# An encoder layer in three-pass fp32: output-projection digits and a merge on VectorE, weights of the down projection loaded straight into kept tiles, PSUM pools reordered

## The chip, the cores and the metric

One core of one Trainium2 chip. The metric is the device time of one execution in microseconds (us). TensorE multiplies, VectorE (DVE), ScalarE (ACT) and GpSimd (POOL) do the elementwise work, and SyncE (SP) issues most DMAs. Each engine takes its instructions strictly in its program's order; semaphores hold an instruction back until what it needs is there.

## What is computed

One layer (x is 1024 rows of 1024 channels, fp32):

```python
h = rmsnorm(x, g_mix)
z = h @ w_in                       # pooling channels | q | k | v
a = pool_mixer(z[pool]) @ w_branch_pool
b = diff_attention(q, k, v) @ w_branch_attn
gates = sigmoid(h @ w_gate + b_gate)
m = gates[pool] * a + gates[attention] * b
y = x + m @ w_out                  # output projection
f = rmsnorm(y, g_ffn)
out = y + relu(f @ w_up) ** 2 @ w_down     # up: 1024 -> 4096, down: 4096 -> 1024
```

## The kernel before

**Digits.** Every fp32 operand is split into two fp32r digits: ScalarE casts the high one (L135) and another engine subtracts it from the source for the low one (L136; VectorE unless the caller names GpSimd). A product is three matmuls in a row, high by high (L142), high by low (L143) and low by high (L144), in `mm3`.

**Seven products.** The large products use Strassen's scheme in Winograd's form: 2 x 2 blocks, seven products numbered "1" to "7", with sums of blocks (S, T, U) formed around them by `add` (L376) and `sub` (L379). Four stages matter here.

- Branch B (`b_product`, L1130 to L1142) makes the attention branch. Its results pass through `merge(d, th, k, eng)` (L1149 to L1153): the gates come in by DMA, ScalarE applies the sigmoid, VectorE multiplies (L1150), and `eng` adds the product to the half row in `mp` (the merged branches m, eight tiles). `merge(i, 1, U2[i], pool)`, four times, stands before the last product "4"; its rows read `mp<-mp,bU`.
- The output projection (`o_product`) multiplies the merged tiles, split into digits by `a_set` (L1158 high, L1159 low; rows `A<-mp`), by the weights. `w_set` loads a product's weights by two calls of `load_rows` (L175): 512 KB each into a raw tile `ro`, from a ring of two; each half is split into `wo`. A product has four such halves, so the seven products have 28 low digits `wo`. The results are in PSUM: oX (products 1, 6 and 3), oY (2 and 5) and oZ (7 and 4), four banks of each at a time. VectorE brings them out by `add` (`y<-oX`, `mp<-oX,xr` with the rows of x). Then come the norm of each row block (`nrs`, L232, L1294; L233 on GpSimd), the scaling `y` (L1299, L1301), the transposes `hb` by TensorE (L1310, eight to a row block, two PSUM banks hbN_0 and hbN_1) and ScalarE's copy out of PSUM (L1338), from which the digits of B11, B21 and the sums BT1 to BT4 are made.
- Up (`u_product`, PSUM tiles X, Y, Z, W) runs over pairs of column blocks of w_up (`wu`, 512 KB each, L1506). The sums `s` of weights (L376, L379) of the first pairs are made while the output projection still runs, and its first loads of `wu` are kept behind the loads of `ro` for products "7" and "4" by `issue_after`.
- Down (`d_product`, PSUM tiles Da and Db) takes quarter blocks: for each product and each q of 8 it loads `ur` (512 KB, L1682) and `wd` (512 KB, L1645), splits both (`u_0h`, `u_0l`, `w_0h`, `w_0l` and so on) and runs 24 matmuls of 128x512. Beside them two sums of weights are kept in SBUF: T1 = b12 - b11, made under product "1" and used in "5" and "6", and T2 = b22 - T1, made in "6" and used in "4". In `t1_made` a block `wdt` is loaded into the ring of raw weights and VectorE subtracts (L379, rows `T<-wdt,wd`), which frees both raw tiles. The raw tiles come from two rings, `prw0` with 2 and `prw1` with 4 tiles of 512 KB; `quarter` chooses between them.

**Order.** The code is traced in program order with priorities, and a list scheduler with a model of the engines writes each engine's final order; a changed engine or pool can therefore move neighbours. Tiles of a pool are reused in turn, and PSUM pools take the banks in the order in which they are opened. `pool_of(mlp_ps, ...)` opens up's PSUM pools after the output projection's banks have been given back.

Of the kernel before, what the change touches and what calls it, by code (L numbers as in the profile page):

```python
# [14 lines left out]
PSUM = bass.MemoryType.PSUM  # L15
# [52 lines left out]
def encoder_kernel(  # L68
# [21 lines left out]
    nc = tc.nc  # L90
# [36 lines left out]
    def raw(shape, name):  # L127
        return rpool.tile(shape, F32, tag="raw", name=name)

    def f(ap):  # L130
        return ap.bitcast(F32)

    def split(hi, lo, src, lo_eng=None):

        made = nc.scalar.copy(hi, src)  # L135
        (lo_eng or nc.vector).tensor_tensor(lo, src, f(hi), op=ALU.subtract)  # L136
        return made
# [34 lines left out]
    def load_rows(src, r0, c0, name, tile_fn):  # L172

        rw = raw([P, 2, 512], f"r{name}")
        loads[name[:2]] = nc.sync.dma_start(rw, src[r0 : r0 + 2 * P, c0 : c0 + 512].rearrange("(kk p) c -> p kk c", p=P))  # L175
        ws = []
        for j in range(2):
            w = tile_fn([P, 2, 512], f"w{name}_{j}")
            split(w[:, 0], w[:, 1], rw[:, j, :], nc.gpsimd)
            ws.append(w)  # L180
        return ws

# [11 lines left out]
    def gate(gts, c):  # L194
        for gt, c0, c1 in gts:
            nc.sync.dma_start(gt, g_dram[c * P : (c + 1) * P, c0:c1])
            nc.scalar.activation(gt, gt, AF.Sigmoid, bias=zero)
# [177 lines left out]
    def add(eng, out_, a, b):  # L375
        eng.tensor_tensor(out_, a, b, op=ALU.add)  # L376

    def sub(eng, out_, a, b):
        eng.tensor_tensor(out_, a, b, op=ALU.subtract)  # L379


    dve, pool = nc.vector, nc.gpsimd
# [38 lines left out]
    with ExitStack() as ph:  # L421
# [83 lines left out]
        act, dve, pol = nc.scalar, nc.vector, nc.gpsimd  # L505
# [487 lines left out]
        for g in range(-2, N + 10):  # L993
# [33 lines left out]
            for tok in ORDER:  # L1027
                if tok not in gens:
                    i = g - tok[1]
# [29 lines left out]
    def tmp(name):  # L1059
        nbank[1] += 1  # L1060
        return fr_tile([P, 512], name) if nbank[1] % 4 in (1, 2) else fo_tile(name)[:, 0:512]
# [24 lines left out]
    def half(d, th):  # L1086
        return mp[d][:, th * 512 : (th + 1) * 512]
# [46 lines left out]
    def b_product(ps, j, i):  # L1134
        c = slice(i * P, (i + 1) * P)
        for d in range(4):
            mm3(
                ps, wa[j][d][:, 0, c], wa[j][d][:, 1, c], *pair(by_[j][d]),
                j in "125" and d == 0, d == 3, j not in "125",
            )  # L1140

    def kept4(name):  # L1142
        ts = [hp0[0].tile([P, S], F32, tag="H", name=f"{name}{i}") for i in range(2)]
        return [ts[i // 2][:, i % 2 * 512 : (i % 2 + 1) * 512] for i in range(4)]

    def merge(d, th, k, eng):
        ga = tmp(f"ga{d}_{th}")
        gate([(ga, th * 512, (th + 1) * 512)], NK + d)
        out_ = ga if k.space == PSUM else k  # L1149
        nc.vector.tensor_tensor(out_, k, ga, op=ALU.mult)  # L1150
        add(eng, half(d, th), half(d, th), out_)
# [40 lines left out]
    U2 = kept4("bU2")  # L1192
# [18 lines left out]
    for i in range(4):  # L1211
        b_product(Z[i], "3", i)
        add(dve, U2[i], Z[i], U2[i])
        merge(i, 1, U2[i], pool)
    for i in range(4):
        b_product(X[i], "4", i)
        merge(i + 4, 0, X[i], dve)
# [8 lines left out]
    def pool_of(stack, name, bufs, space=None, side=None):  # L1226
        kw = {} if space is None else {"space": space}
        return stack.enter_context(
            tc.tile_pool(name=name, bufs=bufs, reuse_waits="tile", side=side, **kw)
        )  # L1230
# [23 lines left out]
    def w_set(j):  # L1254

        src, d0, dh = W_SRC[j]
        room = fw_tile if j in "67" else lambda shape, name: w_tile(shape, name, j not in "23")
        ws = []
        for d in (0, 2):
            ws += load_rows(src, (d0 + d) * P, dh * 512, f"o{j}_{d}", room)  # L1260
        return ws
# [126 lines left out]
    for step in O_TAIL.split():  # L1388
        t = int(step[1])
# [28 lines left out]
    es = pool_of(hs, "es", 2)  # L1418
    mlp_ps = ctx.enter_context(ExitStack())
    by = pool_of(mlp_ps, "by", 1, PSUM)  # L1420
    bm = pool_of(mlp_ps, "bm", 1, PSUM)
    bx = pool_of(mlp_ps, "bx", 1, PSUM)

    def ev(name, shape=(P, 512)):
        return e1.tile(list(shape), F32, tag="ev", name=name)
# [4 lines left out]
    T1s, T2_made = {}, {}  # L1430
# [196 lines left out]
    nraw = [0, 0]  # L1627
# [3 lines left out]
    wd = w_down.rearrange("(q i ab p) c -> ab p q i c", i=2, ab=2, p=P)  # L1631
    NQ = NP // 2
    T1s, T2s = {}, {}

    def kept(tag, q):
        return pd.tile([P, 2, 512], F32, tag=tag, name=f"{tag}_{q}", bufs=NQ)

    def keep(name):
        return pd.tile([P, 512], F32, tag="kp", name=name, bufs=12)

    def quarter(j, q, ab, dh):
        nraw[1] += j not in "1t"
        first = q % 4 < 2 if j == "1" else j != "t" and nraw[1] % 3 == 0
        r = prws[0 if first else 1].tile([P, 2, 512], F32, tag="rw", name=f"wd{j}_{q}_{ab}{dh}")
        nc.sync.dma_start(r, wd[ab, :, q, :, dh * 512 : (dh + 1) * 512])  # L1645
        return r

    def second(j, q):

        if j == "1":  # L1650
            b11[q] = quarter(j, q, 0, 0)
            return b11[q]
        if j == "5":
            return T1s[q]
        if j == "2":
            return quarter(j, q, 1, 0)
        if j == "3":
            return quarter(j, q, 1, 1)
        if j == "6":
            b22 = quarter(j, q, 1, 1)  # L1660
            T2s[q] = kept("T2", q)
            sub(dve, T2s[q], b22, T1s[q])
            return T2s[q]
        if j == "7":
            b22, b12 = quarter(j, q, 1, 1), quarter(j, q, 0, 1)
            sub(dve, b22, b22, b12)
            return b22
        b21 = quarter(j, q, 1, 0)
        sub(dve, b21, b21, T2s[q])
        return b21  # L1670

    b11 = {}

    def t1_made(q):
        b12 = quarter("t", q, 0, 1)
        T1s[q] = kept("T1", q)
        sub(dve, T1s[q], b12, b11.pop(q))

    def operands(j, q):
        nraw[0] += 1  # L1680
        ur = purs[nraw[0] > 2 and nraw[0] % 2].tile([P, 2, 512], F32, tag="ur", name=f"ur{j}_{q}")
        nc.sync.dma_start(ur, ud[SIDES[j][0], q])  # L1682
        out_ = []
        for n, src, pool_ in (("u", ur, puo), ("w", second(j, q), puo if (j, q) == ("1", 0) else pwo)):
            hi, lo = (pool_.tile([P, 2, 512], F32R, tag="op", name=f"{n}{j}_{q}{x}") for x in "hl")
            split(hi, lo, src, dve)
            out_ += [hi, lo]
        return out_
# [11 lines left out]
    def d_product(banks, j, last=False, early={}):  # L1700
        for q in range(NQ - 2 if last else NQ):
            d_step(banks, j, q, early.get(q) or operands(j, q), range(4))
            if j == "1" and q > 1:
                t1_made(q - 2)
        if j == "1":
            t1_made(NQ - 2)
            t1_made(NQ - 1)
        if last:
            ops = {q: operands(j, q) for q in (NQ - 2, NQ - 1)}
            for t in range(4):  # L1710
                for q in ops:
                    d_step(banks, j, q, ops[q], (t,))
# [6 lines left out]
    def with_residual(banks, name, th, dh):  # L1719

        got = []
        for t in range(4):
            k = keep(f"{name}{t}")
            add(dve, k, banks[t], residual(name, 4 * th + t, dh))
            got.append(k)
        return got
# [24 lines left out]
    U2 = with_residual(DX, "U2y", 0, 1)  # L1751
# [42 lines left out]
```

## Time and profile before

| | |
|---|---|
| median of 3 runs | 1525.06 us |
| lowest and highest | 1523.22, 1526.81 us |
| the profiled execution | 1526.86 us |
| its span in the trace | 1525.1 us |
| granted TensorE clock, mean | 0.999 |
| TensorE busy | 1510.0 us, 7590 matmuls and transposes |
| VectorE, ScalarE, GpSimd busy | 1063.1, 809.2, 405.9 us |
| DMA | 247.87 MB, mean 163 GB/s |

Busy times are shares of the span. TensorE's records are pipelined: a 128x512 matmul is listed with 0.39 us and follows the one before in 0.227. A bracket at a row's end gives the idle time of its engine ahead of it and what ended it. In the stage that the change begins with (about 795 to 875 us) the output projection runs, up starts at about 901, and down at about 1213. The last matmul ends at about 1521.

### The profile page before, as it was taken

The numbers are of one execution on the slowest core, as the hardware profiler recorded it, in microseconds if no ns is written. First come the engines' busy times: TensorE is split into PE (matmuls) and PEld (weight loads), VectorE is DVE, ScalarE is ACT, GpSimd is POOL, SyncE is SP. The second block draws the span as 40 slices with busy tenths as digits, with TensorE's granted clock in tenths as the row PEclk, the third lists the DMA queues.
The fourth block names the chain that finished last, engine by engine and source line by source line (L and its number), as shares of the span: only waits on it lengthen the run. The fifth ranks groups of instructions, "written<-read, shape, count | busy, mean of one in ns | idle before, by whom it ended". The sixth has DMA issues, their size and how long they took to land. (4 is left out here: it accounts for less than half of the span.)

```text
span 1525.1 us, 22082 instructions
## 1 busy us (share of the span) xinstructions
PE 1510.0 (99%) x7590; PEld 1308.3 (86%) x7590; DVE 1063.1 (70%) x2138; ACT 809.2 (53%) x1671; POOL 405.9 (27%) x489
## 2 busy tenths in 40 slices
PE   9999999999999999999999999999999999999999
PEld 8999998999999989888887778888888878888887
DVE  7777768887788777745469799667656668556572
ACT  7656565655555564554443477556555624333331
POOL 4545543454436343312447510000000000000000
PEclk9999999999999999999999999999999999999999
DMA  7224333422434244448855734454433899537650
GB/s 227 73 81 125 103 97 106 132 84 78 125 118 150 91 142 149 160 131 277 292 185 192 222 139 137 154 186 155 152 126 111 284 345 360 178 126 261 227 191 28
DMA packets 211211, 247.87 MB, mean 163 GB/s; under 512 B 12981, under 2 KB 146074, under 8 KB 211098
## 3 DMA queue, kind: packets, MB, share of 16 engines
q1 hardware_dynamic: 193530, 219.01, 43.7%
q10 hardware_dynamic: 17568, 27.44, 4.9%
q8 instruction: 60, 0.98, 0.3%
q14 instruction: 53, 0.43, 0.1%
HBM read 172.97 MB, written 73.43 MB: 162 GB/s over the span
## 5 line engine op out<-in xcount | busy, mean ns | idle before, releaser
L144 PE MATMUL z<-wqkv,hT 128*128 128x384 f32 x512 | 174.0, 340 | 0.1
L142 PE MATMUL z<-wqkv,hT 128*128 128x384 f32 x512 | 173.6, 340 | 0.1
L143 PE MATMUL z<-wqkv,hT 128*128 128x384 f32 x512 | 172.9, 338 | 0.0
L794 ACT ACTIVATE s<-s,nm 128x256 f32<-128x256 f32 (+7 forms) x128 | 99.4, 777 | 77.6 <-DVE nm L786 76.8
L716 POOL TENSOR_TENSOR ms<-ms,mhalf 128x4 f32<-128x4 f32 x64 | 71.0, 1110 | 164.7 <-DVE ms L715 160.6
L142 PE MATMUL g<-hT,fwgate 128*128 128x512 f32 x256 | 101.2, 395 | 0.6 <-ACT yps L340 0.4
L144 PE MATMUL g<-hT,fwgate 128*128 128x512 f32 x256 | 100.8, 394 | 0.0
L143 PE MATMUL g<-hT,fwgate 128*128 128x512 f32 x256 | 100.6, 393 | 0.0
L142 PEld LDWEIGHTS z<-wqkv,hT 128*128 128x128 f32 x512 | 96.3, 188 | 3.1 <-ACT hT L445 0.6
L143 PEld LDWEIGHTS z<-wqkv,hT 128*128 128x128 f32 x512 | 96.3, 188 | 2.5 <-DVE wqkv L445 0.3
L144 PEld LDWEIGHTS z<-wqkv,hT 128*128 128x128 f32 x512 | 96.2, 188 | 2.4 <-DVE hT L445 0.6
L786 DVE CUSTOM_DVE_ANT_0 s<-sc,dist 128x512 f32<-128x512 f32 (+3 forms) x128 | 71.8, 568 | 19.5 <-PE sc L784 13.9
L136 DVE TENSOR_TENSOR AS<-s,AS 128x512 fp32r<-128x512 f32 x64 | 43.5, 688 | 33.6 <-ACT AS L135 33.5
L783 PE MATMUL sc<-K,Q 128*128 128x512 f32 (+2 forms) x192 | 66.5, 351 | 0.2 <-DVE nm L786 0.2
L784 PE MATMUL sc<-K,Q 128*128 128x512 f32 (+2 forms) x192 | 65.0, 345 | 0.0
L136 POOL TENSOR_TENSOR wqkv<-rqkv,wqkv 128x384 fp32r<-128x384 f32 x56 | 58.7, 1067 | 23.5 <-ACT wqkv L135 23.2
L136 POOL TENSOR_TENSOR fwgate<-frgate,fwgate 128x512 fp32r<-128x512 f32 x32 | 43.7, 1367 | 58.6 <-ACT fwgate L135 58.5
L142 PEld LDWEIGHTS g<-hT,fwgate 128*128 128x128 f32 x256 | 48.1, 188 | 9.4 <-ACT yps L340 0.7
L144 PEld LDWEIGHTS g<-hT,fwgate 128*128 128x128 f32 x256 | 48.1, 188 | 9.2
L143 PEld LDWEIGHTS g<-hT,fwgate 128*128 128x128 f32 x256 | 48.1, 188 | 8.6
L136 DVE TENSOR_TENSOR AT_0l<-ta,AT_0h 128x512 fp32r<-128x512 f32 (+1 forms) x48 | 31.9, 666 | 30.1 <-ACT AT_0h L135 26.0
L379 POOL TENSOR_TENSOR wd<-wd 128x128 f32<-128x128 f32 (+1 forms) x64 | 50.3, 792 | 8.6 <-ACT wd L981 5.9
(513 smaller groups left out, 4670.6 us busy)
## 6 DMA issues: line engine op xcount, KB each, us to landing
wd<-in_w_down_dram SPq DMA_DIRECT2D x56, 512.0 KB, 5.2
wu<-in_w_up_dram SPq DMA_DIRECT2D x32, 512.0 KB, 4.3
udS<-us SPq DMA_DIRECT2D x64, 256.0 KB, 3.2
ur<-udS SPq DMA_DIRECT2D x32, 512.0 KB, 3.8
rqkv<-in_w_in_dram SPq DMA_DIRECT2D x64, 192.0 KB, 2.9
ur<-ud SPq DMA_DIRECT2D x24, 512.0 KB, 4.6
frgate<-in_w_gate_dram SPq DMA_DIRECT2D x32, 256.0 KB, 2.7
g_dram<-go ACTq DMA_DIRECT2D x32, 256.0 KB, 2.0
```

What stands on the lines that cost most here:

```text
L136: (lo_eng or nc.vector).tensor_tensor(lo, src, f(hi), op=ALU.subtract)
L142: nc.tensor.matmul(ps, lhs_hi, rhs_hi, start=first, stop=False, **kw)
L143: nc.tensor.matmul(ps, lhs_hi, rhs_lo, start=False, stop=False, **kw)
L144: return nc.tensor.matmul(ps, lhs_lo, rhs_hi, start=False, stop=last, **kw)
L379: eng.tensor_tensor(out_, a, b, op=ALU.subtract)
L716: powered[0] = nc.gpsimd.tensor_tensor(ms, ms, mhalf[:, 0:4], op=ALU.pow)
L783: nc.tensor.matmul(dst, Q[:, i, 0, :], rhs, start=True, stop=False)
L784: nc.tensor.matmul(dst, Q[:, i, 1, :], rhs, start=False, stop=True)
L786: nc.vector.tensor_tensor_reduce(out=s[i][:, c : c + w], in0=sc[:, 0:w], in1=dist[:, o0 + c : o0 + c + w], scale=2.0 ** -(h + 1), scalar=B ...
L794: exped[0] = nc.scalar.activation(s[i][:, 0:n], s[i][:, 0:n], AF.Exp, bias=last, scale=-1.0, accum_out=Z[:, i, t : t + 1])
```

## The change

Four edits:

1. `load_rows` names no engine for the low digits, so they go to VectorE.
2. `merge(i, 1, U2[i], ...)` adds on VectorE.
3. Up's PSUM pools are opened in the order by, bx, bm, where it was by, bm, bx.
4. In down, T1 and T2 are loaded straight into the kept tiles by a new helper `load_quarter`, and VectorE subtracts in place; the raw rings no longer hold a block for them, and `quarter` chooses its ring by another count.

```diff
@@ load_rows
-            split(w[:, 0], w[:, 1], rw[:, j, :], nc.gpsimd)
+            split(w[:, 0], w[:, 1], rw[:, j, :])
@@ branch B, product "3"
-        merge(i, 1, U2[i], pool)
+        merge(i, 1, U2[i], dve)
@@ PSUM pools of up
     by = pool_of(mlp_ps, "by", 1, PSUM)
+    bx = pool_of(mlp_ps, "bx", 1, PSUM)
     bm = pool_of(mlp_ps, "bm", 1, PSUM)
-    bx = pool_of(mlp_ps, "bx", 1, PSUM)
@@ down
+    def load_quarter(r, q, ab, dh):
+        nc.sync.dma_start(r, wd[ab, :, q, :, dh * 512 : (dh + 1) * 512])
+
     def quarter(j, q, ab, dh):
-        nraw[1] += j not in "1t"
-        first = q % 4 < 2 if j == "1" else j != "t" and nraw[1] % 3 == 0
+        nraw[1] += j != "1"
+        first = nraw[1] % 3 == 0 if j != "1" else q % 3 == 0
         r = prws[0 if first else 1].tile([P, 2, 512], F32, tag="rw", name=f"wd{j}_{q}_{ab}{dh}")
-        nc.sync.dma_start(r, wd[ab, :, q, :, dh * 512 : (dh + 1) * 512])
+        load_quarter(r, q, ab, dh)
         return r
@@ second, product "6"
-            b22 = quarter(j, q, 1, 1)
             T2s[q] = kept("T2", q)
-            sub(dve, T2s[q], b22, T1s[q])
+            load_quarter(T2s[q], q, 1, 1)
+            sub(dve, T2s[q], T2s[q], T1s[q])
@@ t1_made
-        b12 = quarter("t", q, 0, 1)
         T1s[q] = kept("T1", q)
-        sub(dve, T1s[q], b12, b11.pop(q))
+        load_quarter(T1s[q], q, 0, 1)
+        sub(dve, T1s[q], T1s[q], b11.pop(q))
```

In all 32 rows leave GpSimd's program and 32 join VectorE's; the other engines keep their number of rows. Up's banks are now X of the first product in bank 1, where it was bank 3; the transposes hb4 and hb5 use banks 0 to 3 in both.

On VectorE, in the middle of the output projection, the digits of product "5" and "3" (`wo5`, `wo3`) come between the digits of A for product "6" and the results of oY (the difference of the two orders):

```order
 L1159 TENSOR_TENSOR A6_2_9612<-mp2_8573,A6_2_9612 128x512
+L379 TENSOR_TENSOR mp7_8773<-mp7_8773,mp3_8605 128x512
+L136 TENSOR_TENSOR wo5_0_0_9688<-ro5_0_9686,wo5_0_0_9688 128x512
+L136 TENSOR_TENSOR wo5_0_1_9691<-ro5_0_9686,wo5_0_1_9691 128x512
 L1159 TENSOR_TENSOR A6_3_9615<-mp3_8605,A6_3_9615 128x512
+L136 TENSOR_TENSOR wo5_2_0_9696<-ro5_2_9694,wo5_2_0_9696 128x512
+L136 TENSOR_TENSOR wo5_2_1_9699<-ro5_2_9694,wo5_2_1_9699 128x512
 L376 TENSOR_TENSOR y0_9530<-oY0_9618,y0_9530 128x512
 L376 TENSOR_TENSOR y1_9545<-oY1_9635,y1_9545 128x512
 L376 TENSOR_TENSOR y2_9560<-oY2_9652,y2_9560 128x512
 L1159 TENSOR_TENSOR A5_0_9702<-mp0_8463,A5_0_9702 128x512
+L136 TENSOR_TENSOR wo3_0_0_9780<-ro3_0_9778,wo3_0_0_9780 128x512
```

Six rows (five new digits, and a sum that has moved down) now stand ahead of or between the additions `y<-oY` and the digits of A around them.

On TensorE, at the end of the output projection, the transposes of row block 4 (hb4) move behind the last product into oZ3:

```order
 L143 MATMUL oZ2_10084<-wo4_2_1_9907,A4_3_10007 128x512
 L144 MATMUL oZ2_10084<-wo4_2_1_9907,A4_3_10007 128x512
-L1310 MATMUL hb4_0_10216<-identf_95,y4_10135 128x128 x4
-L1310 MATMUL hb4_1_10217<-identf_95,y4_10135 128x128 x4
 L142 MATMUL oZ3_10162<-wo4_0_0_9896,A4_0_9998 128x512
 L143 MATMUL oZ3_10162<-wo4_0_0_9896,A4_0_9998 128x512
@@ -4517,4 +4515,6 @@
 L143 MATMUL oZ3_10162<-wo4_2_1_9907,A4_3_10007 128x512
 L144 MATMUL oZ3_10162<-wo4_2_1_9907,A4_3_10007 128x512
+L1310 MATMUL hb4_0_10216<-identf_95,y4_10135 128x128 x4
+L1310 MATMUL hb4_1_10217<-identf_95,y4_10135 128x128 x4
 L1310 MATMUL hb5_0_10256<-identf_95,y5_10194 128x128 x4
```

Now hb4 and hb5 stand together behind all of oZ's matmuls.

On SyncE, at the start of down, the queue before, behind the last `ur` of product "1":

```order
L1682 DMA ur1_7_13326<-ud11_7_10338 128x1024
L1716 DMA x1y00_13375<-yd_129 128x512
L1716 DMA x1y10_13379<-yd_129 128x512
L1716 DMA x1y20_13383<-yd_129 128x512
L1645 DMA wd1_4_00_13208<-in_w_down_dram 128x2x512
L1645 DMA wdt_2_01_13242<-in_w_down_dram 128x2x512
L1682 DMA ur2_0_13394<-ud12_0_10339 128x1024
L1645 DMA wd1_5_00_13248<-in_w_down_dram 128x2x512
L1645 DMA wdt_3_01_13282<-in_w_down_dram 128x2x512
L1682 DMA ur2_1_13430<-ud12_1_10340 128x1024
L1645 DMA wd1_6_00_13288<-in_w_down_dram 128x2x512
L1645 DMA wdt_4_01_13322<-in_w_down_dram 128x2x512
```

Each row `wdt` is a load for T1. The queue now, from the same row on:

```order
L1685 DMA ur1_7_13321<-ud11_7_10338 128x1024
L1642 DMA T1_0_13162<-in_w_down_dram 128x2x512
L1642 DMA T1_1_13201<-in_w_down_dram 128x2x512
L1642 DMA T1_2_13240<-in_w_down_dram 128x2x512
L1642 DMA T1_3_13279<-in_w_down_dram 128x2x512
L1642 DMA T1_4_13318<-in_w_down_dram 128x2x512
L1642 DMA T1_5_13357<-in_w_down_dram 128x2x512
L1642 DMA T1_6_13360<-in_w_down_dram 128x2x512
L1642 DMA T1_7_13363<-in_w_down_dram 128x2x512
L1719 DMA x1y00_13367<-yd_129 128x512
L1719 DMA x1y10_13371<-yd_129 128x512
L1642 DMA wd1_6_00_13284<-in_w_down_dram 128x2x512
```

The eight loads for T1 stand together, ahead of `wd1_6` (the seventh weight block of product "1"); `wd1_4` and `wd1_5` have moved ahead of this piece. Further down, the loads for T2 stand between those of product "2".

## The prediction

> **What bounds the kernel now.** The first part of the page comes first:
>
> ```profile
> PE 1510.0 (99%) x7590; PEld 1308.3 (86%) x7590; DVE 1063.1 (70%) x2138; ACT 809.2 (53%) x1671; POOL 405.9 (27%) x489
> ```
>
> TensorE is busy for all but 15 us of the span (1525.1 us), and the change leaves every matmul in the program. It can therefore win no more than the gaps between matmuls, and lose whatever new gap it makes. The list of TensorE's waits names the gaps (total us, times, longest):
>
> ```profile
> PE oX L142 <- DVE mp L376: 2.1, 2, 1.2
> PE Db L142 <- ACT w_0h L135: 1.9, 1, 1.9
> ...
> PE X L142 <- ACT y L1338: 1.0, 1, 1.0
> ...
> PE oY L142 <- ACT A L1158: 0.8, 1, 0.8
> PE oZ L142 <- DVE nrs L232: 0.6, 1, 0.6
> PE hb L1310 <- DVE y L1301: 0.5, 1, 0.5
> PE X L142 <- ACT U L1542: 0.5, 1, 0.5
> ...
> PE oY L144 <- DVE A L1159: 0.3, 1, 0.3
> ```
>
> Seven of these rows lie in 828 to 940 us, from the output projection (oX, oY, oZ) to the first products of up (X), and one is the first matmul of down's second product (Db). Only these are in the reach of the edits. The windows say what the other engines do there (columns: PE, PEld, DVE, ACT, POOL, clock, DMA share, GB/s):
>
> ```profile
> 800.00:900.00 100.00, 96.19 (x436) 77.76 (x435) 89.38 (x121) 46.60 (x95) 52.05 (x36) 1.00 0.59 195
> ...
> 1200.00:1300.00 100.00, 98.14 (x426) 80.74 (x426) 70.45 (x70) 42.35 (x49) 0.00 (x0) 0.98 0.93 337
> 1250.00:1260.00 10.00, 8.14 (x34) 6.30 (x33) 5.89 (x7) 3.86 (x4) 0.00 (x0) 0.93 1.00 353
> 1260.00:1270.00 10.00, 10.00 (x42) 8.19 (x40) 7.00 (x7) 4.03 (x5) 0.00 (x0) 0.90 1.03 384
> ```
>
> In the output projection VectorE is nearly full and GpSimd half busy; at the start of down the DMA engines are full (share 1.00) and every compute engine but TensorE has room. So the two halves of the change meet two different limits.
>
> A wait costs more than its row, because the first matmuls after it are slow to get going. TensorE's timeline around the first oX wait, and the start after the second:
>
> ```profile
> 849.65 0.39 PE L143 MATMUL oX<-wo,A 128*128 128x512 f32 x1
> ...
> 850.56 0.39 PE L144 MATMUL oX<-wo,A 128*128 128x512 f32 x1
> 851.82 0.47 PE L142 MATMUL oX<-wo,A 128*128 128x512 f32 x1 [0.88 <-DVE mp L376]
> 852.13 0.40 PE L143 MATMUL oX<-wo,A 128*128 128x512 f32 x1
> ...
> 864.16 0.47 PE L142 MATMUL oX<-wo,A 128*128 128x512 f32 x1 [1.21 <-DVE mp L376]
> ```
>
> Undisturbed, four spacings take 0.91 us, 0.227 each. From 850.56 to 852.13 two spacings take 1.57 instead of 0.45: 1.12 lost, 0.24 more than the 0.88 of the wait.
>
> **The digits and the merge (first two edits).** 28 low digits `wo` and 4 adds of the merge, 32 instructions of 128x512, go from GpSimd to VectorE. Their price is in the timelines of the two engines:
>
> ```profile
> 817.69 1.75 POOL L136 TENSOR_TENSOR wo<-ro,wo 128x512 fp32r<-128x512 f32 x1
> ```
>
> ```profile
> 818.21 1.78 DVE L1159 TENSOR_TENSOR A<-mp,A 128x512 fp32r<-128x512 f32 x1
> 819.91 0.68 DVE L1150 TENSOR_TENSOR ga<-bX,ga 128x512 f32<-128x512 f32 x1
> 820.51 0.68 DVE L379 TENSOR_TENSOR mp<-mp,mp 128x512 f32<-128x512 f32 x1
> ...
> 868.95 2.88 DVE L1159 TENSOR_TENSOR A<-mp,A 128x512 fp32r<-128x512 f32 x2
> ```
>
> With GpSimd idle such an instruction takes VectorE 0.60 us from start to start (819.91 to 820.51); beside a running `wo` of GpSimd it takes 1.70 (818.21 to 819.91) or 1.4 (the pair at 868.95). So VectorE gains 32 x 0.60 = 19.2 us of work, and each moved instruction takes away one of GpSimd's that could hold up VectorE by 0.8 to 1.1. GpSimd's 52 us in this window are some 30 instructions of 1.75; if two thirds of them meet a two-input operation of VectorE (my estimate), the hold-ups come to 16 to 22 us. VectorE's net load is then -3 to +3 us; I take 0. What does change is the order: a digit now is ready 0.60 us after ScalarE's high digit, not 1.75, and the two-slot ring of raw weights, which the low digit frees, turns faster. Three rows show that this ring paces the queue of SyncE, and through it VectorE and TensorE:
>
> ```profile
> SPq L175 <- POOL wo L136: 27.5, 10, 5.8
> ```
>
> ```profile
> 852.12 0.39 SPq L175 DMA_DIRECT2D ro<-o_sum  x1
> 852.56 0.46 SPq L1506 DMA_DIRECT2D wu<-in_w_up_dram  x1
> ...
> 853.78 0.51 SPq L1506 DMA_DIRECT2D wu<-in_w_up_dram  x1
> ```
>
> ```profile
> 851.00 0.68 DVE L376 TENSOR_TENSOR mp<-oX,xr 128x512 f32<-128x512 f32 x1
> ...
> 861.52 0.69 DVE L376 TENSOR_TENSOR s<-wu 128x512 f32<-128x512 f32 x1 [5.16 <-DMA wu<-in_w_up_dram]
> ```
>
> The load of `ro` at 852.12 stands ahead of up's first weights; the second `wu` leaves at 853.78, lands 7.7 us later, and VectorE stands 5.16 us before it with the eviction of oX in its queue behind it. That is the second oX wait. The first one is the eviction at 851.00, which stood behind digits of A that had been stretched. I followed the changed order row by row with 0.60 per instruction, the casts as before, and each DMA taking as long as before. VectorE then reaches the last digit of oY's first operand 2.3 us sooner than before, 1.2 ahead of its need; the eviction of oX that began at 851.00 begins at 845.1 where 848.8 is needed (850.79, when TensorE was through with what it had, less the 2 us won by then); `wu` leaves at 846 to 847 and lands by 855, so that the eviction behind it starts at 857.4 where 859.7 is needed (864.16 less the 1.37 lost there and the 3.1 won by then). Margins are 1 to 4 us. So oY's two waits, oX's two and oZ's go: 0.8 + 0.3 + 2.1 + 0.6 = 3.8, with 0.24 for each of six, 1.4: 5.2 us.
>
> **The PSUM order (third edit).** The transposes hb4 and hb5 keep PSUM banks 0 to 3, but X of up's first product leaves the bank that it shared with the last transposes (hb5_1, bank 3) for bank 1, that of hb4_1, which is given back sooner; the transposes hb4 and hb5 now stand behind all of oZ's matmuls. The waits of X on ACT y (1.0) and of hb on DVE y (0.5) should go with this and with the earlier y: 1.5 + 2 x 0.24 = 2.0. The wait of X on ACT U (0.5) has the same order as before and stays. By my replay the eviction of hb4_1 ends at 899 where X0 starts at 901.0, the thinnest place. Bounds: 0 if VectorE's chain of `y` is no earlier, 2.0 if it is. I take 1.5. Together with the digits: **6.7 us**, bounds 3 and 7.2.
>
> **Down (fourth edit).** No instruction goes or comes; the 8 + 8 loads of T1 and T2 no longer pass through the rings of raw weights, so they no longer wait for slots. The wait for them, before:
>
> ```profile
> 1226.06 8.21 DMA wd<-in_w_down_dram
> ...
> 1249.44 7.73 DMA wd<-in_w_down_dram
> ...
> 1258.29 1.89 PE Db L142 x4
> ```
>
> ```profile
> 1253.36 1.23 DVE L379 TENSOR_TENSOR T<-wdt,wd 128x1024 f32<-128x1024 f32 x1 [3.94 <-DMA wdt<-in_w_down_dram]
> ```
>
> ```profile
> 1256.05 0.39 PE L144 MATMUL Da<-w_7h,u_7l 128*128 128x512 f32 x1
> 1258.29 1.89 PE L142 MATMUL Db<-w_0h,u_0h 128*128 128x512 f32 x4 [1.86 <-ACT w_0h L135]
> ...
> 1262.74 0.39 PE L142 MATMUL Db<-w_0h,u_0h 128*128 128x512 f32 x1
> ```
>
> The chain runs load, digits, T, next load: the load of w_0 could leave only at 1249.44, as a T freed its slot. TensorE stops, and then runs slowly until 1262: from 1256.05 to 1262.74, 13 spacings take 6.69 where 13 x 0.227 = 2.95, so this place costs 3.74. Half of it is the clock, which the windows show granted at 0.93 and 0.90. [...]
>
> In the changed order SyncE issues all eight T1 loads in one row when the kept tiles come free (1223.4 in the time of before), ahead of the loads of w_6 and w_7 of the first product, and T2 loads stand between those of the second product. The engines carry 512 KB in 1.37 us at 384 GB/s, 1.49 at 353, 1.56 at 337 (rows above). A product's step of 24 matmuls takes 24 x 0.227 = 5.44, so the first product began 8 x 5.44 ahead of 1256.3, at 1212.8. Counting 512-KB units behind 1223.4, with some 2 us for the first to land: w_6 is the 11th, lands by 1241 and is needed with its digits by 1245.4; w_0 of the second product is the 17th or so, lands by 1250 and is needed at 1256.3; its w_1 is at 24.5 units, lands at 1258.9, 1261.8 or 1263.5 by the three rates, plus 1.05 for its cast, and is needed at 1261.7. So the wait of Db goes, and one at the next step takes its place: 0, 1.2 or 3.4 us. I take 1.2, of the middle rate, as both windows with full DMA engines bear it. Gain 3.74 - 1.2 = **2.5**, bounds 0 and 3.7.
>
> **Sum.** 6.7 + 2.5 = 9.2 us off the profiled execution's 1526.86, which is 1.8 above the median of the runs (1525.06) and within their spread; taken off the median: 1515.8. What moves less than 0.2% (3 us) a measurement of this kernel can hardly tell from no change.
>
> **Rivals.** (a) *The loads of T1 and T2 are in the way.* The DMA share of 1.00 speaks for it, and so does that 16 loads are pulled ahead of needed ones in one queue. [...] The count above has them in this order already, so it decides from 1.56 us a load: then w_1 costs 3.7 with its slow clock and down gains nothing: 1525.06 - 6.7 = 1518.4. Against it: 353 and 384 GB/s in the very place.
>
> (b) *The waits move on.* VectorE is at 89 of 100 us; if its net load is +3 and not 0, the margins of 1 to 2 us at oX and X0 are gone, two of the waits come back, and up's first steps wait for their digits instead: of the 6.7, 3 stay; with down's 2.5 minus up to 1: 1520.5. For it: the thin places. [...]
>
> (c) *The change does nothing that is seen:* the ring was not the pace, since `ro` lands late whoever frees it, and down's wait comes back one step on: within 3 us, 1524.
>
> (d) *Slower: VectorE takes over GpSimd's waits.* GpSimd stood idle ahead of its `wo` until ScalarE had a landed load to cast:
>
> ```profile
> 823.77 4.98 POOL L136 TENSOR_TENSOR wo<-ro,wo 128x512 fp32r<-128x512 f32 x3 [4.33 <-ACT wo L135]
> 832.82 6.41 POOL L136 TENSOR_TENSOR wo<-ro,wo 128x512 fp32r<-128x512 f32 x4 [4.07 <-ACT wo L135]
> ...
> 858.67 2.54 POOL L136 TENSOR_TENSOR wo<-ro,wo 128x512 fp32r<-128x512 f32 x2 [4.76 <-ACT wo L135]
> 864.86 6.42 POOL L136 TENSOR_TENSOR wo<-ro,wo 128x512 fp32r<-128x512 f32 x4 [3.64 <-ACT wo L135]
> ```
>
> Now the digit stands in VectorE's queue, and behind it the evictions that free oX and oY for TensorE. If the four waits of 16.8 us in all come over, and each has 2 us of margin, 8.8 us of gaps appear and the 6.7 don't go: 1525.06 + 8.8 - 2.5 = 1531.4. It decides where a `ro` lands more than 11 us after its issue, not 7.7 as the `wu` beside it did, or where the order has a digit ahead of an eviction that is due before it. Against it: in the replay ScalarE's cast comes before VectorE reaches the digit in all places but those with margin.
>
> **How the numbers follow.** Forecast 0.50, (a) 0.13, (b) 0.17, (c) 0.10, (d) 0.10. Faster by over 0.2% is the forecast with (a) and (b), 0.80; the same is (c), 0.10; slower is (d), 0.10. The range leaves out (c) and (d): its low end has all bounds at their best (7.2 + 3.7, and 1 us of run to run, 1513.2), its high end is (b) with down's gain gone, 1522.
>
> **What would show it.** Right: in the profile after, the list of TensorE's waits has lost oX <- mp, oY, oZ, hb and X <- y; GpSimd has no row between 800 and 870 but the nrs; VectorE's L1159 rows are 0.68 throughout; the `s<-wu` of 861.52 has no wait over 2 us; Db <- w_0h is gone and a shorter Db <- w_1h stands there. Wrong: VectorE waiting on ACT wo or on DMA ro with oX <- mp behind it (d); a wait of Da or Db for w_6h or w_1h of over 3 us (a); new waits for digits of up between 900 and 950 (b). A time over 1522 would mean that one of these took a size that no row here gives.

## The result and the profile after

The changed kernel takes 1515.70 us (median of 6 runs, 1514.81 to 1516.14), the kernel before 1524.16 us (6 runs, 1522.84 to 1526.81). The ratio is 0.9943, with a 95% interval of 0.9930 to 0.9955: 8.5 us faster. The forecast was 1515.8 us. The span of the profiled execution fell from 1525.1 to 1514.1 us, by 11.0, more than the times did; why, the last experiment shows: the profile before was of an execution with larger waits than most.

The list of TensorE's waits in the changed kernel, its first three rows (total us, times, longest):

```profile
PE warm L445 <- POOL inv L215: 1.1, 1, 1.1
PE ta L839 <- DVE AT L136: 0.8, 1, 0.8
PE X L142 <- ACT U L1542: 0.4, 1, 0.4
```

The first two lie before 560 us and stood in the kernel before too, among the rows of its list that were left out. Of the eight rows that the prediction lists from the output projection, up and down, one is left, X <- ACT U, the one whose order the change did not touch. The windows (PE, PEld, DVE, ACT, POOL, clock, DMA share, GB/s):

```profile
800.00:900.00 100.00, 100.00 (x466) 83.25 (x465) 93.40 (x165) 51.61 (x113) 4.68 (x8) 1.00 0.61 208
...
1200.00:1300.00 100.00, 100.00 (x442) 82.79 (x442) 76.36 (x73) 42.96 (x46) 0.00 (x0) 1.00 0.93 351
1220.00:1230.00 10.00, 10.00 (x46) 8.28 (x45) 8.61 (x8) 2.11 (x2) 0.00 (x0) 1.00 1.04 404
1250.00:1260.00 10.00, 10.00 (x46) 8.28 (x45) 10.00 (x10) 5.13 (x5) 0.00 (x0) 1.00 1.04 413
```

From 800 to 900 VectorE now executes 165 instructions, 44 more, in 4 us more of busy time (93.40 for 89.38). At the start of down the DMA engines move 404 to 413 GB/s. VectorE's timeline in the output projection:

```profile
820.17 0.69 DVE L1159 TENSOR_TENSOR A<-mp,A 128x512 fp32r<-128x512 f32 x1
...
828.59 1.89 DVE L1159 TENSOR_TENSOR A<-mp,A 128x512 fp32r<-128x512 f32 x3
...
843.83 0.68 DVE L376 TENSOR_TENSOR mp<-oX,xr 128x512 f32<-128x512 f32 x1
...
854.24 0.69 DVE L376 TENSOR_TENSOR s<-wu 128x512 f32<-128x512 f32 x1 [1.72 <-DMA wu<-in_w_up_dram]
```

The digits of A (L1159) follow each other in 0.60 us, three take 1.89, and from 818 us on none takes 1.78 any more. The first copy `mp<-oX,xr` starts 7.2 us sooner than before, `s<-wu` 7.3 us sooner, with a wait of 1.72 in place of 5.16. At the start of down:

```profile
1216.57 4.57 SPq L1642 DMA_DIRECT2D T<-in_w_down_dram  x8
```

```profile
1251.27 1.06 ACT L135 CAST w_1h<-wd 128x1024 fp32r<-128x1024 f32 x1 [5.92 <-DMA wd<-in_w_down_dram]
```

```profile
1253.51 1.22 DVE L136 TENSOR_TENSOR w_1l<-wd,w_1h 128x1024 fp32r<-128x1024 f32 x1
```

```profile
1254.45 1.07 PE L142 MATMUL Db<-w_1h,u_1h 128*128 128x512 f32 x4
1255.36 0.39 PE L143 MATMUL Db<-w_1l,u_1h 128*128 128x512 f32 x1
```

The eight loads of T1 leave in one row. The block w_1 of the second product, at which a new wait was forecast, is cast over at 1252.3; its first matmul runs at 1254.5, without a wait. Its low digit is over at 1254.7 and is needed at 1255.4, because four matmuls with the high digit come first. So w_1 is in time by 0.6 us only.

### The profile page after: what moved, and what is told of

Same layout as the page of the kernel before. It is cut to its first block, busy times and chain, and to the rows that moved or that the text cites. A ratio compares the mean times of both kernels' runs of the same rounds, so it can differ in the third digit from the quotient of the medians.

```text
span 1514.1 us, 22055 instructions
## 1 busy us (share of the span) xinstructions
PE 1506.0 (99%) x7590; PEld 1308.1 (86%) x7590; DVE 1062.3 (70%) x2170; ACT 809.3 (53%) x1671; POOL 352.5 (23%) x457
## 4 chain that ended last, share of the span: by engine, by line
PE 96%; DMA 1%; ACT 1%; DVE 1%; issue 1%; SPq 0%; POOL 0%; DVEq 0%; ACTq 0%; POOLq 0%
PE z L144 5%; PE z L142 5%; PE z L143 5%; PE Da L143 4%; PE Da L142 4%; PE Da L144 4%; PE g L142 4%; PE g L144 4%; PE g L143 4%; PE X L142 3%; PE X L144 3%; PE Db L143 3%; PE Db L142 3%; PE X L143 3%; PE Db L144 3%; PE sc L783 2%
```

## The experiments

Two lengths of the trace tell where a kernel gains or loses: from the first matmul of oX to the first of X on B11 (output projection to up), and from the first of Da to the first of Db on w_1 (down's first product and one step of the second). Neither depends on when the stage began. What a kernel loses in a stage is its length less that of the changed kernel (84.5 and 49.0 us). The times come from four sets of runs, in which the kernel before had medians of 1524.16, 1524.30, 1523.75 and 1523.40 us; between rows of different sets, less than 1 us says nothing. Each ratio below is to the kernel before in the same set.

| kernel | time, us | oX to X, us | Da to Db's w_1, us |
|---|---|---|---|
| before, first profile | 1524.16 | 92.0 | 52.7 |
| before, second profile | 1524.24 (one run) | 90.6 | 51.4 |
| changed | 1515.70 | 84.5 | 49.0 |
| digits alone | 1517.93 | 85.3 | 49.6 |
| merge alone | 1523.29 | 90.6 | 50.3 |
| PSUM order alone | 1523.30 | 90.1 | 50.8 |
| down alone | 1522.63 | 90.7 | 49.0 |
| changed, GpSimd busy | 1531.78 | 100.1 | 49.0 |
| changed, two more loads | 1521.02 | 84.5 | 54.4 |
| changed, T1 straight only | 1515.41 | 84.5 | 49.0 |
| changed, T2 straight only | 1529.88 | 84.5 | 62.5 |
| before, wu earlier | 1521.25 | 88.5 | 53.5 |
| changed, PSUM order of before | 1516.66 | 85.3 | 49.0 |

### The edits one by one

Each of four kernels has one edit of the diff and nothing else.

> The first edit alone: the 28 low digits wo on VectorE, all else as before. My theory: GpSimd's reads no longer hold up VectorE's two-input operations, so the waits of oY, oX and oZ go, some 5.2 us of gaps in TensorE's timeline, and with the earlier y the wait of hb too (0.7); X <- ACT y (1.0 us and its 0.24) and Db <- w_0h (3.7 with the slow clock) stay. Time 5 to 6 us under the kernel before. Rival, the digits in VectorE's own queue do the harm that the other edits hide: under 3 us gained. Rival, the four adds of the merge matter too: one of the two oY waits stays, 4 us gained.

Measured: 1517.93 us, ratio 0.9957 (0.9942 to 0.9972), 6.4 us under the 1524.30 that the kernel before took beside it. All waits of oY, oX, oZ and hb are gone. What is left in the list:

```profile
PE X L142 <- ACT y L1338: 0.7, 1, 0.7
...
PE Db L143 <- DVE w_0l L136: 0.3, 1, 0.3
```

The wait of X stays, shorter. The wait of Db did not stay at 1.9 as expected: here it is 0.3 for the low digit, though SyncE's order of down is that of the kernel before. So the first edit alone is worth most of the whole.

> The second edit alone: four adds of the merge on VectorE. My theory: they lie at 803 to 818 us, where TensorE did not wait, and GpSimd goes on with the digits; VectorE gets 2.4 us more work and about as much less hold-up, the waits of oY and oX stay within 0.5 us of what they were: no change, within 1 us. Rival, the adds ran on the path to the first digits of oY's operand: the oY waits go, 2 us gained.

Measured: 1523.29 us, ratio 0.9997 (0.9988 to 1.0006). No change, as expected; the waits of oY (0.8) and oX (1.4) are there.

> The third edit alone: only the PSUM banks of up's tiles change, every engine's order is that of before. My theory: the wait of X on ACT y (1.0 us, 1.26 with its restart) goes, as X no longer stands behind the last copy out of hb5_1; nothing else changes: 1 to 1.3 us gained in the trace, which the times can hardly show. Rival, the copies out of hb and VectorE's y are late by themselves: the wait comes back in the next product of up, nothing gained.

Measured: 1523.30 us, ratio 0.9991 (0.9982 to 1.0001). X <- ACT y is gone from the list, and nothing came in its place; from oX to X it takes 0.6 us less than the kernel with the merge alone, and 0.5 less than the second profile of the kernel before. The times can't tell it from no change.

> The fourth edit alone: T1 and T2 loaded straight into the kept tiles. My theory: the wait of Db for w_0h and the slow clock behind it go, 3.7 us, and no other wait comes in its place as the loads now run at over 400 GB/s; the seven waits of the output projection stay. Time 3.7 us under the kernel before. Rival, the gain in the kernel with all edits came through down's earlier start: a wait of Db stays here, under 2 us gained.

Measured: 1522.63 us, ratio 0.9989 (0.9980 to 0.9999): 1.7 us, half of what was expected. In the trace no wait of Da or Db is left, and the length is 49.0 us: nine steps of 5.44, all that can be had. The kernels without this edit show 49.6 to 53.5 there, in most of them less than in the first profile (52.7).

### Are VectorE's hold-ups the cause, or the ring of raw weights?

The digits' move does two things: GpSimd hardly works beside VectorE any more (busy 52.05 us of 100 before, 4.68 after, from 800 to 900), and the ring is freed sooner. This kernel leaves the low digits on VectorE, as the changed kernel does, and brings GpSimd's work back. It has all edits, and additions on GpSimd whose results nobody reads.

```diff
+    spare = pr1.tile([P, 2, 512], F32, tag="rw", name="spare")
+    nc.gpsimd.memset(spare[:, 0], 0.0)
...
             ws += load_rows(src, (d0 + d) * P, dh * 512, f"o{j}_{d}", room)
+            for _ in range(2):
+                add(pool, spare[:, 1], spare[:, 0], spare[:, 0])
```

> The changed kernel with 28 additions of 128x512 on GpSimd, from about 800 us on, that nobody waits for (they read and write a spare raw tile of up). Hold-ups theory (GpSimd's reads of SBUF hold up VectorE's instructions with two inputs in SBUF): with the digits now on VectorE too, each addition of 1.3 to 1.75 us costs VectorE 0.8 to 1.1, 22 to 30 us in all between 800 and 850; VectorE was 93% full there, so oY and oX wait for it again, at least the 5 us of the kernel before are lost: 1521 us or more. Rival, what counted was only that the ring of raw weights is given back sooner: the time stays within 1 us of the changed kernel's 1515.7.

Measured: 1531.78 us, ratio 1.0053 (1.0038 to 1.0068), 16 us over the changed kernel. TensorE's list, and the two engines' timelines:

```profile
PE oX L142 <- DVE mp L376: 4.0, 1, 4.0
PE oY L144 <- DVE A L1159: 3.8, 1, 3.8
PE oY L142 <- ACT A L1158: 2.7, 1, 2.7
```

```profile
816.21 39.42 POOL L376 TENSOR_TENSOR spare<-spare 128x512 f32<-128x512 f32 x28
```

```profile
819.48 1.52 DVE L376 TENSOR_TENSOR mp<-mp,ga 128x512 f32<-128x512 f32 x1
820.92 1.53 DVE L136 TENSOR_TENSOR wo<-ro,wo 128x512 fp32r<-128x512 f32 x1
822.37 1.52 DVE L1159 TENSOR_TENSOR A<-mp,A 128x512 fp32r<-128x512 f32 x1
823.82 1.52 DVE L379 TENSOR_TENSOR mp<-mp 128x512 f32<-128x512 f32 x1
825.27 0.68 DVE L1150 TENSOR_TENSOR ga<-bX,ga 128x512 f32<-128x512 f32 x1
825.87 0.92 DVE L136 TENSOR_TENSOR wo<-ro,wo 128x512 fp32r<-128x512 f32 x1
```

While GpSimd adds, VectorE's instructions with two inputs in SBUF start 1.45 us apart, not 0.60; the one with an input in PSUM (825.27) keeps its 0.60, and the one right behind it (825.87) takes 0.84. The waits of oY and oX come back, larger than in the kernel before. VectorE now has the digits as well, and GpSimd adds without a pause; which of the two makes them larger was not tested. Beside such a stream the digits on VectorE do not pay.

The experiment does not hold the ring fixed: as VectorE makes the digits later, two loads of `ro` that leave at 833.5 and 835.3 in the changed kernel leave at 848.2 and 852.5 here. But the trace keeps the two apart. VectorE has no idle time over 0.06 us from 795.4 to 854.3, past both waits of oY, so it waited for no load; and the waits end with digits of A and a copy out of oX, not with a `wo`. The same holds in the kernel before: from 812.2 to 841.5 VectorE stands still only once, for 0.14 us, and oY's waits (829.4 and 830.7) lie in that time. So the rival that only the ring counted does not hold for oY's waits.

That the ring and SyncE's queue count too, the next kernel shows. It is the kernel before, with up's first loads released by the first load for product 7:

```diff
+            loads.setdefault(f"first{j}", loads[f"o{j}"])
...
-                    later.enter_context(tc.issue_after(loads["o4" if p else "o7"].ins))
+                    later.enter_context(tc.issue_after(loads["o4" if p else "first7"].ins))
```

> The kernel before, with up's first two loads kept behind the first load of ro for product 7 and no longer behind the second: they leave some 7 us sooner, as in the changed kernel, while the digits stay on GpSimd. Theory: the second wait of oX (0.5 to 1.2 us) came from VectorE standing before wu with the copy out of oX behind it, so it goes or falls under 0.3; the first wait of oX and those of oY come from held-up digits and stay: 0.7 to 1.5 us less of gaps in the trace, within the spread of the times. Rival, both oX waits come from held-up digits alone: both stay.

Measured: 1521.25 us, ratio 0.9984 (0.9975 to 0.9994). Its list:

```profile
PE Db L142 <- ACT w_0h L135: 2.6, 1, 2.6
...
PE oX L142 <- DVE mp L376: 0.9, 1, 0.9
...
PE oY L142 <- ACT A L1158: 0.8, 1, 0.8
```

```profile
852.90 0.92 DVE L376 TENSOR_TENSOR s<-wu 128x512 f32<-128x512 f32 x1 [0.19 <-DMA wu<-in_w_up_dram]
```

One wait of oX is left of two. VectorE's `s<-wu` waits 0.19 us here, 5.16 before; the scheduler also put that instruction five places sooner, which the experiment could not keep apart from the load. The first wait of oX and oY's stay, with GpSimd's digits. The waits of oZ (0.6) and hb (0.5) are not in this list either, and X <- ACT y is 0.7 and not 1.0. So the earlier load, with the place of `s<-wu`, takes the second oX wait and the later waits of oZ and hb away, though GpSimd still makes the digits: 2.1 of the 5.2 us that the digits' move gives between oX and X (88.5 and 85.3, against 90.6 in the second profile of the kernel before). The waits that stay, oY's and the first of oX, are left to the hold-ups; no kernel here takes away the hold-ups alone.

### Which loads matter in down

> The changed kernel with T1 loaded straight, T2's block loaded through the ring of raw weights as before. Theory: only T1's loads held the ring where TensorE waited (Db <- w_0h), so the time is that of the changed kernel within 1 us and no wait of Db or Da is listed. Rival, T2's loads matter: a wait of 0.5 us or more comes in the second product or in the sixth.

The edit against the changed kernel:

```diff
+            b22 = quarter(j, q, 1, 1)
             T2s[q] = kept("T2", q)
-            load_quarter(T2s[q], q, 1, 1)
-            sub(dve, T2s[q], T2s[q], T1s[q])
+            sub(dve, T2s[q], b22, T1s[q])
```

Measured: 1515.41 us (1515.27 to 1515.68), no wait of Da or Db. T1 alone does it, and no kernel of these is faster than the changed one by more than the times can tell. With T2 back in the ring, w_1 is cast over 8.9 us before its first matmul; in the changed kernel it was 2.1. So T2's straight loads gain nothing here and take up the margin at w_1.

> The changed kernel with T2 loaded straight, T1's block through the ring with the ring's choice as before. Theory: Db waits for w_0h or w_0l as in the kernels without the fourth edit, 0.3 to 1.9 us, and the time is 0.5 to 2.5 us over the changed kernel's. Rival: the ring's pressure comes from T2's loads; no wait, same time as the changed kernel.

The edit against the changed kernel (and the rule of `quarter` as before):

```diff
+        b12 = quarter("t", q, 0, 1)
         T1s[q] = kept("T1", q)
-        load_quarter(T1s[q], q, 0, 1)
-        sub(dve, T1s[q], T1s[q], b11.pop(q))
+        sub(dve, T1s[q], b12, b11.pop(q))
```

Measured: 1529.88 us, ratio 1.0041 (1.0026 to 1.0056): neither theory, but 14 us over the changed kernel and 6 over the kernel before. Its list:

```profile
PE Db L142 <- ACT w_0h L135: 5.7, 1, 5.7
PE Da L142 <- ACT w_6h L135: 3.8, 1, 3.8
```

```profile
1220.65 9.43 SPq L1642 DMA_DIRECT2D T<-in_w_down_dram  x8
1230.62 0.67 SPq L1642 DMA_DIRECT2D wd<-in_w_down_dram  x1
```

```profile
1240.87 1.04 ACT L135 CAST w_6h<-wd 128x1024 fp32r<-128x1024 f32 x1 [1.86 <-DMA wd<-in_w_down_dram]
```

In its order the eight loads of T2, free of the ring, stand in SyncE's queue ahead of wd1_6 (1230.62), which lands 10.2 us after it leaves. The wait for w_6h is rival (a) of the prediction, in a kernel that is nearly the changed one: loads that are not needed yet, in front of one that is. The second wait, for w_0h, lies where the kernel before had its own, behind T1's use of the ring; how much of its 5.7 us the T2 loads add was not separated.

> The changed kernel with two more 512-KB loads into spare tiles, one ahead of the first and one ahead of the second T1 load. Theory, SyncE's loads are served in the order of issue at 404 to 413 GB/s, 1.28 us each: everything behind comes 2.56 us later. In the changed kernel the digits of w_1 of the second product came 0.5 to 1 us before TensorE needed them (high cast over at 1252.3, low at 1254.7, first matmul at 1254.5), so now Db waits for w_1 by 0.4 to 1.5 us, 0.5 to 2 us slower in the trace. Rival, later loads pass earlier ones or the rate rises: no wait of Db.

The edit against the changed kernel:

```diff
         T1s[q] = kept("T1", q)
+        if q < 2:
+            load_quarter(pd.tile([P, 2, 512], F32, tag="more", name=f"more{q}", bufs=2), q, 0, 1)
         load_quarter(T1s[q], q, 0, 1)
```

Measured: 1521.02 us, 5.3 over the changed kernel. The waits are not where they were expected:

```profile
PE Da L142 <- ACT w_7h L135: 1.9, 1, 1.9
PE Da L143 <- DVE w_7l L136: 1.4, 1, 1.4
```

```profile
1242.42 1.04 ACT L135 CAST u_2h<-ur 128x1024 fp32r<-128x1024 f32 x1 [3.51 <-PE Da L143]
1243.37 1.04 ACT L135 CAST w_7h<-wd 128x1024 fp32r<-128x1024 f32 x1
```

The scheduler did not keep the order: besides the two new loads, two `ur` and two T2 loads came to stand ahead of wd1_7, six more 512-KB loads in all. The cast of w_7 starts 39.0 us behind Da's first matmul, 31.1 in the changed kernel: 7.9 us for six loads, 1.32 each, a little of it the cast of u_2h that stands ahead of it. This fits loads that are served in the order of issue, at the price that the rates give (512 KB at 408 GB/s are 1.29 us), but the margin at w_1 that this kernel was to measure was not measured.

### The PSUM order within the whole, and the kernel before once more

> The changed kernel without the third edit; every engine's order is that of the changed kernel, only the PSUM banks differ. Theory: X waits for ACT y again, 0.7 us as with the digits alone (0.9 with its restart), nothing else: 1516.5. Rival, the earlier y has made the shared bank free in time: no wait, same time as the changed kernel.

Measured: 1516.66 us (1515.90 to 1517.08); X <- ACT y is listed with 0.7 us, and oX to X is 0.9 longer. As expected. No hb wait is listed here, nor with the digits alone, nor in the kernel before with `wu` earlier: that wait did not hang on the banks.

> The kernel before, profiled once more. Theory: the waits that end with a DMA landing differ from execution to execution (oX <- mp 1.3 to 2.1 us, Db <- w_0h 0.7 to 1.9 in the kernels run so far), and the first profile had them at their largest; now they are smaller, and the span 1520 to 1523 us. Those that end with an engine (oY, oZ, hb, X) repeat within 0.2. Rival: the waits are fixed by the program; oX 2.1 and Db 1.9 again.

Measured: a span of 1522.5 us; its list begins

```profile
PE Db L142 <- ACT w_0h L135: 1.8, 1, 1.8
PE oX L142 <- DVE mp L376: 1.5, 2, 0.9
...
PE X L142 <- ACT y L1338: 1.0, 1, 1.0
PE oY L142 <- ACT A L1158: 0.8, 1, 0.8
```

The oX waits are 1.5 and not 2.1 (the second of them is behind `wu`). Of those that end with an engine, X (1.0), oY (0.8) and oZ (0.6) repeat; that of hb, 0.5 in the first profile, is missing, which was not expected. Db waits 1.8, nearly as in the first profile, against 0.7 and 1.2 in the kernels with the merge and the PSUM order alone; the latter has every engine's order as before. In these three, and with the digits alone, the load of w_0 leaves 36.1 us behind Da's first matmul, and lands 6.0 (digits), 7.2 (merge), 7.7 (PSUM order) and 8.3 us (this one) later: the wait goes with the landing of one load. Why it lands sooner or later stays open.

Here Db's wait costs 2.4 us and not 3.7, as TensorE runs on at full clock (granted 1.00 from 1250 to 1260 and from 1260 to 1270), with 0.23 us from matmul to matmul after 1258.52:

```profile
1256.92 1.21 PE L142 MATMUL Db<-w_0h,u_0h 128*128 128x512 f32 x4 [1.80 <-ACT w_0h L135]
1258.18 0.50 PE L143 MATMUL Db<-w_0l,u_0h 128*128 128x512 f32 x1
1258.52 0.39 PE L144 MATMUL Db<-w_0h,u_0l 128*128 128x512 f32 x1
1258.75 0.40 PE L143 MATMUL Db<-w_0l,u_0h 128*128 128x512 f32 x1
```

## Why the prediction was right, and where it was not

**The digits.** Right in mechanism: the 0.60 us on VectorE, the hold-ups that go, the ring and `wu`. VectorE's busy time from 800 to 900 rose by 4.0 us, a little over the bound of 3, with some 7 us more of the program in that window. All five waits went, and hb's with them. The row at 819.91, from which the prediction read 0.60, has an input in PSUM; the rows behind it (820.51, 821.11), with both inputs in SBUF and GpSimd idle, show 0.60 too. The sum was set against the first profile: 6.7 forecast with the PSUM order, 7.5 between the two profiles (92.0 to 84.5). Against the second profile of the kernel before it is 6.1. The digits alone give 5.2 of the 6.1, as forecast; some 2.1 can be had by an earlier `wu` alone. The merge, put together with them, adds nothing that times or traces show.

**The PSUM order.** Taken at 1.5, it is 0.9 within the whole and 0.5 to 0.6 alone. The term was mis-sized: it counted the wait of hb, which goes without this edit, with the digits or with `wu` earlier, and was missing in the second profile before.

**Down.** The wait of Db went as forecast. The step that failed is the new wait at w_1, 1.2 us: none came. The price per load was the mis-sized term. I took 1.49 us from the 353 GB/s of a window in which loads still left one by one as slots came free, and the engines, with loads queued ahead, gave 400 to 413, 1.27 to 1.31 us. Counted from T1's first load, the middle rate puts w_1's landing at 1255.0 in the changed kernel; it landed at 1251.2, and at that w_1 is in time. It was close: the count stopped at the cast, and the low digit behind it had 0.6 us to spare. The other error went the opposite way: 3.74 us for the wait of Db is what one execution paid. Over the six profiles with down's code as before, two of the kernel before and four of other kernels, it is 0.6 to 4.5 us, 2.4 on average (the lengths of the table less 49.0: 3.7, 2.4, 0.6, 1.3, 1.8 and 4.5). So 3.74 less 1.2 came out near the measured gain by two errors that cancel, which is luck.

**The sum.** 6.1, from one pair of profiles, and 2.4, a mean of six, are 8.5, which is the difference of the medians; the edit of down alone gave 1.7 in the times, so an agreement to 0.1 is luck too. The forecast subtracted 9.2 from a median of three runs, 1525.06; six runs have 1524.16, and 9.2 would have been 0.7 too much. The time of 1515.8 was thus met more closely than its terms were.

**The rivals.** (a) did not decide here, but the kernel with T2 alone straight, 14 us slower, shows that it can: there it made the wait for w_6h. It is the order of SyncE's queue, not the fourth edit's idea, that keeps it away. That the loads are served in the order of issue, as the count has it, was the author's estimate; it fits the kernel with more loads, where six more of them ahead put the cast of w_7 off by 7.9 us, 1.32 for each. (c) fell with the 8.5 us. (b) and (d) did not come: VectorE waited for ScalarE's casts for 0.72, 0.50 and 0.36 us and never long enough to hold up TensorE.

## What to carry to other kernels

An elementwise step that moves from GpSimd to a nearly full VectorE can be almost free, if GpSimd's work beside it was what made VectorE full: here 44 more instructions took 4 us more of VectorE's time (93.40 for 89.38 of 100), as those of 1.70 us beside GpSimd's went back to 0.60. Look whether anything else on GpSimd stays beside it; with 28 additions there the changed kernel was 16 us slower. Ask also which loads the step sets free: here a load that left earlier gave, by itself, two fifths of what the move gave. Loads taken out of a ring are free to run ahead, and can then stand in SyncE's queue in front of loads that are due (with T2 alone straight, wd1_6 landed 10.2 us after it left, behind eight of them, and TensorE waited 3.8 us for its digit): look at the queue's order, not at the ring. A wait that ends with a DMA, or hangs on one as that of hb did, is a sample (oX 2.1 and 1.5 us, hb 0.5 and none, in two profiles of one kernel); before its size goes into a sum, take it from more than one profiled execution.

## What the runs showed of the hardware

VectorE's 128x512 instructions with both inputs in SBUF take 1.45 us from start to start beside a GpSimd that adds without pause (the first behind one with an input in PSUM 0.84 to 1.37), 1.70 beside a `wo` of GpSimd in the kernel before, 0.60 alone, and GpSimd's own additions take 1.41 (39.42 for 28); with one input in PSUM VectorE keeps 0.60. GpSimd's instructions here read SBUF and write it; which of the two holds VectorE up was not separated, so the "reads" of the expectations are the author's estimate.

TensorE's clock: in the first profile of the kernel before, the wait of 1.86 us was followed by some 3.4 us at about half pace (0.43 us from matmul to matmul, not 0.227; granted 0.93 and 0.90 in two windows of 10 us, 0.7 and 1.0 us lost). One of 1.80 at the same instruction in another execution was followed by none (granted 1.00 in both windows), and one of 2.59 (`wu` earlier) lies in a window of 10 us with 0.83, again 1.7 us lost. So waits of nearly one length, 1.86 and 1.80 us, came with the loss and without it; what decides it was not shown.
